# Retention's query and key projections moved into the seven-product run, kept in DRAM, with attention and retention stepped together

## The chip, the cores and the metric

One core of one Trainium2 chip runs the whole program. The metric is the device time of one launch in microseconds (us). Before the change the median of three runs is 2574.4 us (2571.2 to 2575.66).

## The reference, cut to what matters

Two transformer blocks over 1024 tokens of width 1024, in float32. The change concerns the first block's mixer:

```python
proj = h @ w_in[l]
aq, ak, av, rq, rk, rv, rg, ga, gr = jnp.split(proj, offsets, axis=-1)
att = sliding_window_attention(aq, ak, av, sinks)          # 8 heads of 64, window 128
ret = retention_chunkwise(rq, rk, rv)                      # 4 heads, key 128, value 256, chunks of 128
ret = head_group_norm(ret, ret_gn_gain[l]) * jax.nn.silu(rg)
merged = jax.nn.sigmoid(ga) * (att @ w_att_o[l]) + jax.nn.sigmoid(gr) * (ret @ w_ret_o[l])
...
# retention, per head and chunk
scores = jnp.einsum('bihd,bjhd->bhij', qi, ki) * decay_intra
o = jnp.einsum('bhij,bjhv->bihv', scores, vi) + jnp.einsum('bihd,bhdv->bihv', qi, state) * decay_q
state = decay_chunk * state + jnp.einsum('bjhd,bjhv->bhdv', ki * decay_k, vi)
```

## The kernel before, in words

Every large product is made of float32r matmuls of 128 by 128 by 512, three for each product, since each operand is split into a high and a low part (`split`, L277: ScalarE casts the high part at L279, VectorE subtracts at L281). Engines: PE is TensorE, DVE VectorE, ACT ScalarE, POOL GpSimd, and SP the queue that issues nearly all DMAs. Instructions of one engine run in program order. A tile is waited for by semaphores that the framework places.

Most projections use a seven-product (Strassen-like) form of a 2 by 2 block product. `s_run` (L504) does this for pairs of 128 output columns: seven groups of 12 matmuls (`s_group`, L496), 84 a pair, with the weights' combinations made by DVE (`s_emits`, L399) and an `ev` callback for each of the four output blocks. The activation operands of the seven products are held in `X.keep` (`Rows`, L118). Block 1 (`block1`, L772) sends 15 pairs through it: the gates RG, GA and GR, and the attention's queries and keys AQ1, AK and AQ0 (L838, L839).

Retention's queries and keys are not among them. After `s_run` each of the eight units rq0, rk0, ... rk3 is a plain product (`t_unit`, L587, with `t_group`, L573): two halves of 24 matmuls, 384 in all. For them the operand's high and low parts of a block more than the seven products need are kept (the order ending in 8, L741, and the loop at L745).

The rest is written as generators. `pump` (L232) starts `self.new` of those that stand in `self.pend`, then lets each older one take its next step, newest first. `t_group` pumps once in the middle of 24 matmuls and `t_unit` once behind them, so a step of attention or of retention comes after each 12 matmuls.

- `att1_quad` (L1272): four heads of one 128-query tile in four steps: scores (8 matmuls, then for each head a reduction on DVE, L1285, and an exponential on ACT, L1288); transposes (L1301) with copies by ACT (L1304) and DVE (L1306); the product with V (L1314); transposes back and the split of the result (L1323 to L1328). 16 quads, all of u = 0 first.
- `retention` (L1336): `vload`, eight `chunk` steps in two halves each (scores and key transpose L1355 to L1361; then output, state and statistics L1369 to L1384), and `finish` (loads of the gate rows L1394, normalisation L1397, transposes L1404, result rows L1406). `queue_retention` (L1331) puts two heads side by side, heads 0 and 1 after rk1, heads 2 and 3 after rk3.

Then the loop at L902 multiplies the attention's result by w_att_o: 16 half units of 12 matmuls (`ao`), each gated at L911 and stored, each followed by a pump. Then follows the seven-product run with w_ret_o (`d_run` at L953, evacuation `ro_evac` L937), whose operands are retention's result rows (`a_split`, L1109).

Buffers that matter: four PSUM banks for `mm`, `sc`, `po`, `tq` and `ao` (pool `pm`), three for transposes (`pt`), one for `pv`, and 43 SBUF slots of 4 KB a partition (`S`). Weights are loaded into two raw buffers (`load_raw`, L294) and split `ahead` pieces in advance in `tick` (L321).

Of the kernel before, what the change touches and what calls it, by code (L numbers as in the profile page):

```python
# [117 lines left out]
class Rows:  # L118
# [32 lines left out]
    def queue(self, c, order, kept=False):  # L151

        k = self.k
        k.d_queue(None, [(c, 0, 4, order[1:], kept)])
# [6 lines left out]
    def half(self, kt, th):  # L161
        hi, lo = self.keep[{(0, 0): 1, (1, 0): 2, (0, 1): 8, (1, 1): 4}[kt // 4, th]][kt % 4 // 2]
        return hi[:, kt % 2, :], lo[:, kt % 2, :]
# [12 lines left out]
class Kern:  # L176
# [165 lines left out]
    def t2_chunk(self, wa, ca, wb, cb, keys):  # L342

        def load(s):
            return lambda r: r.rearrange("p (k s c) -> p k s c", k=8, s=2)[:, :, s, :]
        va = wa[:, ca : ca + P].rearrange("(k p) c -> p k c", p=P)
        vb = wb[:, cb : cb + P].rearrange("(k p) c -> p k c", p=P)
        ck = self.add_chunk([(load(0), va), (load(1), vb)])
        for u, key in enumerate(keys):
            def src(hi, lo, r, u=u):  # L350
                return hi, lo, r.rearrange("p (k s c) -> p k s c", k=8, s=2)[:, :, u, :]
            self.add_piece(key, ck, [P, 8, P], src)

# [150 lines left out]
    def s_run(self, op, pairs, at={}):  # L504
# [4 lines left out]
        saved = {}  # L509
        def hoist2(i):  # L510
# [76 lines left out]
    def t_unit(self, w, X, evac, kts=range(8)):  # L587
        for half in range(2):
            ps = self.PM("mm")
            self.t_group(ps, w, X, half, kts)  # L590
            self.tick()
            evac(half, ps)
            self.pump()

# [40 lines left out]
    def plan(self):  # L635
# [49 lines left out]
    def run(self):  # L685
# [55 lines left out]
        X.queue("rv", ORD_V + (8,), kept=True)  # L741
# [3 lines left out]
        while len(X.keep) < 8:  # L745
            self.a_split(True)
            if ("rv", 8, 1) in self.a_ready:
                X.keep[8] = [self.a_ready.pop(("rv", 8, j)) for j in range(2)]
        self.flush()
# [22 lines left out]
    def block1(self, X):  # L772
# [19 lines left out]
        aq_d = {(t, th): dp.tile([P, 2, 512], F32, name=f"aq_d{t}_{th}") for t in (2, 3) for th in range(2)}  # L792
        self.dk = self.cp.tile([P, 4], F32, name="dk")

        def tables():
# [4 lines left out]
            nc.sync.dma_start(self.dk, a["c_main"][:, 9 * P :])  # L800
            alibi = [self.S(f"alibi{i}") for i in range(2)]
# [36 lines left out]
        pairs = [(f"{k}{i}", gate_ev(k, i)) for k in ("RG", "GA", "GR") for i in range(0, 8, 2)]  # L838
        pairs += [("AQ1", aq_ev(1)), ("AK", ak_ev), ("AQ0", aq_ev(0))]  # L839
        self.s_run(X.ops, pairs)  # L840
        tables()
        self.ahead = 1
# [14 lines left out]
        self.pend.append(av_tr())  # L857
        for u in range(2):
            for n in range(NT):
                self.pend.append(self.att1_quad(n, u, aq, ak, av, att))  # L860

# [3 lines left out]
        qk = []  # L865
        for h in range(4):
            qd, kT = self.S("qd"), self.S("kT")

            def q_ev(half, ps):
                nc.vector.tensor_tensor(  # L870
                    qd[:, 512 * half : 512 * half + 512].rearrange("p (c i) -> p c i", i=P),
                    ps.rearrange("p (c i) -> p c i", i=P),
                    self.dq[h][:, None, :].to_broadcast([P, 4, P]), ALU.mult)

            self.t_unit(self.get(f"rq{h}"), X, q_ev)
            if h == 0:
                for t in (2, 3):
                    aq[t] = {}
                    for th in range(2):
                        aq[t][th] = q = self.S("qst", [P, 2, 512], F32R)  # L880
                        nc.sync.dma_start(q.bitcast(F32), aq_d[t, th])
            self.t_unit(self.get(f"rk{h}"), X, lambda half, ps: nc.scalar.copy(kT[:, 512 * half : 512 * half + 512], ps))
            qk.append((qd, kT))
            if h % 2:
                self.queue_retention((h - 1, h), qk, rg_d, rows)
                self.new = 2
# [8 lines left out]
        def gload(i):  # L895
            t = self.S("tga")
            nc.sync.dma_start(t, ga_d[i])
            return t
        tga = gload(0)
        while att.missing:  # L900
            self.pump()
        for i in range(8):  # L902
            if i % 2 == 0:
                ao = self.get(f"ao{i // 2}")
            st, tg, tga = self.S("m1"), tga, gload(i + 1) if i < 7 else None
            for half in range(2):
                sl = slice(512 * half, 512 * half + 512)
                po = self.PM("ao")
                self.t_group(po, ao, att, half, range(4), cs=P * (i % 2))
                self.tick()  # L910
                nc.vector.scalar_tensor_tensor(st[:, sl], tg[:, sl], 1.0, po, op0=ALU.add, op1=ALU.mult)  # L911
                if i >= 5:
                    self.ahead = 2
                    self.a_split()
                self.pump()
            nc.sync.dma_start(m_d[i], st)
# [63 lines left out]
    def ffn1(self, X, x1_d):  # L980
# [64 lines left out]
        self.s_run(X.ops, pairs, {  # L1045
# [4 lines left out]
        X.keep.clear()  # L1050
# [221 lines left out]
    def att1_quad(self, n, u, aq, ak, av, att):  # L1272
# [24 lines left out]
        for s in range(2):  # L1297
# [33 lines left out]
    def queue_retention(self, heads, qk, rg_d, rows):  # L1331
        parts = [self.retention(h, *qk[h], rg_d, rows) for h in heads]
        for gens in zip(*parts):
            self.pend.extend(gens)

    def retention(self, h, qd, kT, rg_d, rows):  # L1336
        nc = self.nc
        v = []
# [4 lines left out]
        def vload():  # L1343
            for b in range(2):
                t = self.S("rvh", [P, 4, 256])
                nc.sync.dma_start(
# [577 lines left out]
```

## Time and profile before

| what | value |
|---|---|
| median of three runs | 2574.4 us |
| the profiled execution's own time | 2574.72 us |
| its span, first to last instruction | 2572.9 us |
| mean granted TensorE clock | 0.988 |
| PE busy | 2504.7 us (97%) |
| DVE busy | 1765.6 us (69%) |
| ACT busy | 1142.2 us (44%) |
| matmuls recorded | 11857 |

Times in the rows count from the span's first instruction. A matmul's record is longer than its share of the engine, because matmuls overlap in the array; the distance from one start to the next is what one costs. The granted clock is 1.00 at 2.4 GHz and 0.50 at 1.2 GHz.

### The profile page before, as it was taken

Reading aid. Unit: us, or ns where it says so; the run is one execution under the profiler, and the core shown is the slowest. Engines: PE = TensorE matmul, PEld = TensorE weight load, DVE = VectorE, ACT = ScalarE, POOL = GpSimd, SP = SyncE. Lnnn points to the kernel's source line nnn. Section 1 sums busy time; section 2 is a strip of 40 time slices with the busy share of each in tenths; the row PEclk is TensorE's granted clock in tenths of the full one; section 3 lists DMA queues with packets and bytes.
Section 4 is the critical chain, followed back from the end, with each engine's and each line's share of the span. In section 5 each row is a group of like instructions: output and inputs, shape, how many; then the busy total and the mean of one; then the engine's idle time right before and its main releaser. Section 6 shows DMA issues by size and latency. Waiting matters only on the chain.

```text
span 2572.9 us, 31324 instructions
## 1 busy us (share of the span) xinstructions
PE 2504.7 (97%) x11857; PEld 2073.0 (81%) x11857; DVE 1765.6 (69%) x2789; ACT 1142.2 (44%) x2068; POOL 178.7 (7%) x236
## 2 busy tenths in 40 slices
PE   7999999999999999999999999999999999899998
PEld 5888888888787888878788777888887888788886
DVE  7664456556899755555799986666558444478888
ACT  5444445412425433333333644566436555553334
POOL 1000000000002000000000300002421000000006
PEclk9999999999999999999999999999899999999999
DMA  4333333135343122233433415221242333522334
GB/s 157 104 110 103 123 103 107 39 113 185 109 186 131 66 70 87 87 130 98 174 121 131 144 49 172 102 81 51 81 160 82 104 117 103 180 108 81 115 123 147
DMA packets 178703, 291.57 MB, mean 113 GB/s; under 512 B 10168, under 2 KB 84552, under 8 KB 178552
## 3 DMA queue, kind: packets, MB, share of 16 engines
q1 hardware_dynamic: 178552, 289.57, 33.1%
q8 instruction: 93, 1.52, 0.2%
q14 instruction: 58, 0.48, 0.1%
HBM read 212.89 MB, written 80.31 MB: 114 GB/s over the span
## 4 chain that ended last, share of the span: by engine, by line
PE 78%; DVE 13%; DMA 3%; ACT 3%; issue 2%; POOL 1%; SPq 0%; DVEq 0%; ACTq 0%; POOLq 0%
PE da L1201 6%; PE a L500 6%; PE a L502 6%; PE a L501 6%; PE da L1200 6%; PE da L1199 6%; PE db L1201 3%; PE db L1200 3%; PE db L1199 3%; PE b L502 3%; PE b L501 3%; PE b L500 3%; DVE wl L281 3%; PE pv L1861 2%; DVE midl L281 2%
## 5 line engine op out<-in xcount | busy, mean ns | idle before, releaser
L500 PE MATMUL a<-midh,ws 128*128 128x512 f32 x708 | 276.8, 391 | 9.1 <-DVE f L1669 8.0
L502 PE MATMUL a<-midh,ws 128*128 128x512 f32 x708 | 276.4, 390 | 0.0
L501 PE MATMUL a<-midl,ws 128*128 128x512 f32 x708 | 276.4, 390 | 0.0
L1201 PE MATMUL da<-wh,midl 128*128 128x512 f32 x624 | 245.1, 393 | 6.6 <-DVE midl L281 6.6
L1200 PE MATMUL da<-wl,midh 128*128 128x512 f32 x624 | 244.6, 392 | 3.4 <-DVE wl L281 3.4
L1199 PE MATMUL da<-wh,midh 128*128 128x512 f32 x624 | 246.0, 394 | 0.6 <-ACT midh L279 0.6
L279 ACT CAST midh<-mt 128x1024 fp32r<-128x1024 f32 x80 | 82.9, 1036 | 244.6 <-DVE mt L1142 81.3
L1201 PE MATMUL db<-wh,midl 128*128 128x512 f32 x436 | 171.0, 392 | 3.5 <-DVE midl L281 3.5
L1200 PE MATMUL db<-wl,midh 128*128 128x512 f32 x436 | 170.8, 392 | 2.2 <-DVE wl L281 2.2
L1199 PE MATMUL db<-wh,midh 128*128 128x512 f32 x436 | 171.1, 392 | 1.4 <-ACT midh L279 1.4
L500 PEld LDWEIGHTS a<-midh,ws 128*128 128x128 f32 x708 | 133.4, 188 | 38.7 <-issue 8.9
L501 PEld LDWEIGHTS a<-midl,ws 128*128 128x128 f32 x708 | 133.5, 189 | 27.7
L502 PEld LDWEIGHTS a<-midh,ws 128*128 128x128 f32 x708 | 133.5, 189 | 27.7
L279 ACT CAST ws<-tc 128x512 fp32r<-128x512 f32 x180 | 111.4, 619 | 88.3 <-DVE tc L414 87.1
L1201 PEld LDWEIGHTS da<-wh,midl 128*128 128x128 f32 x624 | 117.8, 189 | 34.5 <-DVE midl L281 10.3
L1200 PEld LDWEIGHTS da<-wl,midh 128*128 128x128 f32 x624 | 117.9, 189 | 29.0 <-DVE wl L281 4.8
L500 PE MATMUL b<-midh,ws 128*128 128x512 f32 x360 | 140.1, 389 | 0.0
L501 PE MATMUL b<-midl,ws 128*128 128x512 f32 x360 | 140.1, 389 | 0.0
L502 PE MATMUL b<-midh,ws 128*128 128x512 f32 x360 | 140.0, 389 | 0.0
L279 ACT CAST wh<-raw 128x1024 fp32r<-128x1024 f32 x121 | 120.6, 1037 | 42.0 <-DMA raw<-in_w_ff_dram 15.2
L1199 PEld LDWEIGHTS da<-wh,midh 128*128 128x128 f32 x624 | 118.0, 189 | 26.0 <-issue 1.2
L281 DVE TENSOR_TENSOR wl<-raw,wh 128x1024 fp32r<-128x1024 f32 x117 | 136.2, 1197 | 3.6 <-ACT wh L279 3.5
(348 smaller groups left out, 5822.8 us busy)
## 6 DMA issues: line engine op xcount, KB each, us to landing
raw<-in_w_ff_dram SPq DMA_DIRECT2D x31, 1024.0 KB, 5.4
mid_d<-f SPq DMA_DIRECT2D x108, 256.0 KB, 2.1
midr<-mid_d SPq DMA_DIRECT2D x52, 512.0 KB, 6.9
raw<-in_w_in_dram SPq DMA_DIRECT2D x22, 1024.0 KB, 5.4
x<-x_d SPq DMA_DIRECT2D x24, 512.0 KB, 4.5
raw<-in_w_up_dram SPq DMA_DIRECT2D x11, 1024.0 KB, 5.6
raw<-in_w_gate_dram SPq DMA_DIRECT2D x10, 1024.0 KB, 5.5
xt<-in_x_dram SPq DMA_DIRECT2D x16, 512.0 KB, 10.9
```

Source lines behind the costliest of these rows:

```text
L279: self.nc.scalar.copy(hi, s)
L281: e.tensor_tensor(lo, s, hi.bitcast(F32), ALU.subtract)
L500: nc.tensor.matmul(ps, hi[:, i], xh, start=(first and i == 0), stop=False, skip_group_check=True)
L501: nc.tensor.matmul(ps, hi[:, i], xl, start=False, stop=False, skip_group_check=True)
L502: nc.tensor.matmul(ps, lo[:, i], xh, start=False, stop=(i == 3), skip_group_check=True)
L1199: nc.tensor.matmul(ps, xh, wh, start=(kt == 0 and p in (1, 5, 2)), stop=False, skip_group_check=True)
L1200: nc.tensor.matmul(ps, xh, wl, start=False, stop=False, skip_group_check=True)
L1201: nc.tensor.matmul(ps, xl, wh, start=False, stop=(kt == m - 1), skip_group_check=True)
L1861: nc.tensor.matmul(pv[:, 64 * x : 64 * x + 64], pT[0:w, 2 * x + e, :], vv[:, 64 * h : 64 * h + 64], start=(e == 0), stop=(e == 1))
```

## The change

- The four heads' query and key units become four pairs RQ0 to RQ3 of `s_run`, between GR and AQ1. Their `ev` (`rqk_ev`) multiplies the query block by its decay and stores both to DRAM (`rq_d`, `rk_d`); `t_unit`, `t2_chunk` and the eighth operand go.
- The decay tables are loaded at pair 11, the alibi tables at the last pair, the queries of u = 1 right behind `s_run`.
- `retention` loads keys, queries and values from DRAM in two halves (`load(0)`, and `load(1)` at chunk 2); its gate rows are loaded a step earlier. The scaled key goes from DVE to ACT, and so does the second transposed copy of `att1_quad`.
- Quads and chunks go into `pend` in threes (one quad, one chunk of each of two heads, the chunks two pumps behind), in the order half, u, n, and `self.new` is 3.
- The `ao` loop takes half 0 of all eight columns first, and starts when that half's quads are done. Until its twelfth group no weights of w_ret_o are split (`cap`).
- `s_run` drops each kept operand after its last use, in all three places that call it.

```diff
+        pairs += [(f"RQ{h}", w_in, O_RQ + P * h, O_RK + P * h) for h in range(4)]
...
-        for h in range(4):
-            self.t2_chunk(w_in, O_RQ + P * h, w_in, O_RK + P * h, [f"rq{h}", f"rk{h}"])
...
-        X.queue("rv", ORD_V + (8,), kept=True)
+        X.queue("rv", ORD_V)
...
+        def rqk_ev(h):
+
+            def ev(th, c, ps, add):
+                f, src = self.H("f"), ps
+                if add is not None:
+                    nc.vector.tensor_tensor(f, ps, add, ALU.add)
+                    src = f
+                if c == 0:
+                    nc.vector.tensor_tensor(
+                        f.rearrange("p (c i) -> p c i", i=P), src.rearrange("p (c i) -> p c i", i=P),
+                        self.dq[h][:, None, :].to_broadcast([P, 4, P]), ALU.mult)
+                elif add is None:
+                    nc.scalar.copy(f, ps)
+                nc.sync.dma_start((rk_d if c else rq_d)[h][:, 512 * th : 512 * th + 512], f)
+            return ev
...
-        self.s_run(X.ops, pairs)
-        tables()
-        self.ahead = 1
+        self.s_run(X, pairs, {11: decays, 18: tables})
+        for t in (2, 3):
+            aq[t] = {}
+            for th in range(2):
+                aq[t][th] = q = self.S("qst", [P, 2, 512], F32R)
+                nc.sync.dma_start(q.bitcast(F32), aq_d[t, th])
+        self.ahead = 2
...
-            self.t_unit(self.get(f"rq{h}"), X, q_ev)
...
-            self.t_unit(self.get(f"rk{h}"), X, lambda half, ps: nc.scalar.copy(kT[:, 512 * half : 512 * half + 512], ps))
...
+        ret = [self.retention(h, rq_d[h], rk_d[h], rg_d, rows) for h in range(4)]
+        chunks = [[ret[h][c] for h in (2 * g, 2 * g + 1)] for g in range(2) for c in range(10)]
+        quads = [self.att1_quad(4 * half + n, u, aq, ak, av, att) for half in range(2) for u in range(2) for n in range(4)]
+        lag, none = 2, iter(())
+        self.pend.extend([av_tr(), none, none])
+        for i in range(lag + 20):
+            self.pend.append(quads[i] if i < 16 else none)
+            self.pend.extend(chunks[i - lag] if i >= lag else [none, none])
+        self.new = 3
...
+        for g in range(16):
+            half, i = divmod(g, 8)
+            while any(2 * n + u in att.missing for n in range(4 * half, 4 * half + 4) for u in range(2)):
+                self.pump()
+            if i // 2 not in ao:
+                ao[i // 2] = self.get(f"ao{i // 2}")
...
+            if g >= 11:
+                self.cap = 10 ** 9
+                self.a_split()
             self.pump()
...
-            dst = pT[:, 2 * nh * s : 2 * nh * (s + 1), :]
-            if s == 0:
-                nc.scalar.copy(dst, tp[:, : 2 * nh, :])
-            else:
-                nc.vector.tensor_copy(dst, tp[:, : 2 * nh, :])
+            nc.scalar.copy(pT[:, 2 * nh * s : 2 * nh * (s + 1), :], tp[:, : 2 * nh, :])
...
+        def load(b):
+
+            t, v = self.S("rkq", [P, 2, 512]), self.S("rvh", [P, 4, 256])
+            for i, src in enumerate((rk_d, rq_d)):
+                nc.sync.dma_start(t[:, i, :], src[:, 512 * b : 512 * b + 512])
...
         def chunk(c):
...
+            if c == 2:
+                load(1)
...
-                nc.vector.tensor_scalar(sd[:, 1, :], tp[:, 1, :], self.dk[:, h : h + 1], None, op0=ALU.mult)
+                nc.scalar.activation(sd[:, 1, :], tp[:, 1, :], AF.Copy, scale=self.dk[:, h : h + 1])
```

## Rows read from the trace of the kernel before

**Rows 1.** The page's head and its line of PE (busy us, share, instructions).
```profile
span 2572.9 us, 31324 instructions
PE 2504.7 (97%) x11857; PEld 2073.0 (81%) x11857; DVE 1765.6 (69%) x2789; ACT 1142.2 (44%) x2068; POOL 178.7 (7%) x236
```

**Rows 2.** Busy time by stretch: from:to, us, each engine's busy us, PEclk, DMA share, GB/s.
```profile
107.70:394.06 286.36, 286.34 (x1264) 236.57 (x1263) 153.65 (x238) 127.53 (x220) 0.00 (x0) 1.00 0.33 108
394.06:569.00 174.94, 174.74 (x1063) 151.56 (x1062) 101.94 (x342) 64.41 (x211) 4.51 (x4) 1.00 0.24 71
569.00:644.20 75.20, 72.86 (x369) 61.90 (x367) 52.91 (x126) 15.06 (x26) 3.67 (x4) 1.00 0.57 200
659.00:684.00 25.00, 21.22 (x91) 16.56 (x90) 24.70 (x27) 6.96 (x8) 0.00 (x0) 1.00 0.10 36
684.00:691.00 7.00, 6.59 (x16) 5.19 (x17) 5.83 (x6) 3.91 (x5) 0.00 (x0) 0.53 0.00 1
1683.60:1696.30 12.70, 11.34 (x59) 9.47 (x57) 9.81 (x32) 10.37 (x31) 0.00 (x0) 0.73 0.18 58
```

**Rows 3.** Timeline of SP in the gate pairs: start us, us, instruction.
```profile
304.67 0.32 SPq L788 DMA_DIRECT2D GR_d<-g  x1
...
342.75 0.32 SPq L788 DMA_DIRECT2D GR_d<-g  x1
```

**Rows 4.** Timeline of PE, one attention step between two blocks of twelve matmuls.
```profile
428.11 0.63 PE L1263 MATMUL sc<-kst,qst 128*128 128x256 f32 x4
...
430.03 1.90 PE L1314 MATMUL pv<-av,pT 128*128 128x64 f32 x16
...
431.91 0.48 PE L581 MATMUL mm<-midh,wh 128*128 128x512 f32 x1
...
434.75 0.52 PE L1263 MATMUL sc<-kst,qst 128*128 128x256 f32 x3
```

**Rows 5.** Timeline of PE, one retention step of two heads between such blocks.
```profile
529.65 0.38 PE L1355 MATMUL tp<-qd,kT 128*128 128x128 f32 x2
...
532.72 0.58 PE L581 MATMUL mm<-midh,wh 128*128 128x512 f32 x1
...
535.65 0.38 PE L1355 MATMUL tp<-qd,kT 128*128 128x128 f32 x2
```

**Rows 6.** Timeline of DVE behind the seven-product run, up to the first quad's reductions.
```profile
394.73 0.68 DVE L810 TENSOR_TENSOR f<-a,p 128x512 f32<-128x512 f32 x1
...
398.88 1.40 DVE L1236 TENSOR_TENSOR qst<-f,qst 64x512 fp32r<-64x512 f32 x2 [0.69 <-ACT qst L1233]
...
403.79 0.34 DVE L1285 CUSTOM_DVE_ANT_0 z<-sc,alibi,nsink 128x128 f32<-128x128 f32 x1
```

**Rows 7.** Timeline of PE where the second block's attention begins.
```profile
1683.66 0.55 PE L1263 MATMUL sc<-kst,qst 128*128 128x256 f32 x1
...
1696.29 1.29 PE L1263 MATMUL sc<-kst,qst 128*128 128x256 f32 x4
```

**Rows 8.** Groups of 394 to 644 us: busy us, mean ns | idle before, releaser.
```profile
L1288 ACT ACTIVATE z<-z,nm 128x256 f32<-128x256 f32 x56 | 27.8, 497 | 33.7 <-DVE nm L1285 33.7
...
L1285 DVE CUSTOM_DVE_ANT_0 z<-sc,alibi,nsink 128x256 f32<-128x256 f32 x56 | 23.7, 480 | 28.0 <-PE sc L1268 28.0
...
L1383 DVE BATCH_NORM_STATS2 bs<-ro 128x6 f32<-128x256 f32 x32 | 13.7, 428 | 16.2 <-ACT ro L1381 16.2
...
L1381 ACT COPY ro<-po 128x256 f32<-128x256 f32 x32 | 11.9, 372 | 82.9 <-DVE st L1378 56.0 <-DVE st L1376 18.9 <-PE po L1371 8.0
...
L1378 DVE SCALAR_TENSOR_TENSOR st<-st,po 128x256 f32<-128x256 f32 x24 | 9.7, 406 | 6.3 <-PE po L1373 6.3
...
L1306 DVE COPY pT<-tp 128x512 f32<-128x512 f32 x14 | 9.2, 659 | 0.0
...
L1304 ACT COPY pT<-tp 128x512 f32<-128x512 f32 x14 | 7.9, 565 | 2.2 <-PE tp L1301 2.2
```

**Rows 9.** Timeline of PE behind the last chunk: idle time and its releaser in brackets.
```profile
640.13 0.66 PE L1404 MATMUL tp<-ident,ro 128*128 128x128 f32 x4 [1.72 <-DVE rrow L1406]
```

**Rows 10.** Timeline of DVE where the run with w_ret_o reaches its second product.
```profile
659.02 0.69 DVE L949 TENSOR_TENSOR mg<-db,mg 128x512 f32<-128x512 f32 x1 [1.51 <-PE db L1201]
```

More of the change, by code (lines that the diff above doesn't have):

```diff
@@ L502, in s_group, with s_run, op @@
             nc.tensor.matmul(ps, lo[:, i], xh, start=False, stop=(i == 3), skip_group_check=True)
-    def s_run(self, op, pairs, at={}):
+    def s_run(self, X, pairs, at={}):
         nc = self.nc
         saved = {}
+        used = dict.fromkeys(range(1, 8), 0)
+        def op(p):
+            used[p] += 1
+            ops = X.ops(p)
+            if used[p] == len(pairs):
+                del X.keep[p]
+            return ops
         def hoist2(i):
@@ L585, in t_group @@
                 self.pump()
[L587 to L593, printed above, removed]
     def m_group(self, ps, X, t, ws, mid=None):
@@ L893, in block1, with gload @@
         self.a_ok = lambda k0, p: self.ret_heads <= (2 if p == 1 else 0) if k0 == 0 else left[0] <= {1: 12, 2: 8}.get(p, 0)
-        def gload(i):
-            t = self.S("tga")
-            nc.sync.dma_start(t, ga_d[i])
-            return t
-        tga = gload(0)
-        while att.missing:
-            self.pump()
[L902 to L916, printed above, removed]
+        def gload(g):
+            half, i = divmod(g, 8)
+            t = self.S("tga", [P, 512])
+            nc.sync.dma_start(t, ga_d[i][:, 512 * half : 512 * half + 512])
+            return t
+        tga, ao = gload(0), {}
+        self.cap = next(i for i, p in enumerate(self.pieces) if p[0] == "ro:1_0")
+        for g in range(16):
+            half, i = divmod(g, 8)
+            while any(2 * n + u in att.missing for n in range(4 * half, 4 * half + 4) for u in range(2)):
+                self.pump()
+            if i // 2 not in ao:
+                ao[i // 2] = self.get(f"ao{i // 2}")
+            st, tg, tga = self.S("m1", [P, 512]), tga, gload(g + 1) if g < 15 else None
+            po = self.PM("ao")
+            self.t_group(po, ao[i // 2], att, half, range(4), cs=P * (i % 2))
+            self.tick()
+            nc.vector.scalar_tensor_tensor(st, tg, 1.0, po, op0=ALU.add, op1=ALU.mult)
+            nc.sync.dma_start(m_d[i][:, 512 * half : 512 * half + 512], st)
+            if g >= 11:
+                self.cap = 10 ** 9
+                self.a_split()
+            self.pump()
+        ao.clear()
         self.new = 1
@@ L1044, in ffn1 @@
         self.d_queue(mid_d, [(k0, k0, m, ORD_M, False) for k0, m in self.dchunks])
-        self.s_run(X.ops, pairs, {
+        self.s_run(X, pairs, {
             n - 7: self.bias_build,
@@ L1328, in att1_quad, with retention @@
         nc.vector.tensor_tensor(lo[:, :, o : o + P], tp[:, 0:2, :], hi[:, :, o : o + P].bitcast(F32), ALU.subtract)
[L1331 to L1336, printed above, removed]
+    def retention(self, h, rq_d, rk_d, rg_d, rows):
         nc = self.nc
-        v = []
+        kqv, sg = {}, []
         gc = float(np.exp(RET_LOG_G[h] * 128.0))
@@ L1370, in chunk @@
             if c > 0:
-                nc.tensor.matmul(po, qd[:, cs], st["S"], start=False, stop=True)
+                nc.tensor.matmul(po, qd, st["S"], start=False, stop=True)
             if c < 7:
@@ L1410, in finish @@
             self.ret_heads -= 1
-        return [vload()] + [chunk(c) for c in range(8)] + [finish()]
+        return [first()] + [chunk(c) for c in range(8)] + [finish()]
     def bias_build(self):
@@ L1690, in ffn2 @@
         self.d_queue(mid_d, [(k0, k0, m, ORD_M, False) for k0, m in self.echunks])
-        self.s_run(X.ops, pairs, {
+        self.s_run(X, pairs, {
             len(pairs) - 3: lambda: self.pend.append(self.d_first()),
```

77 lines of the change are left out of this document (19 added, 58 removed).

## The prediction

> **What bounds the kernel now.** I read the page's head first: PE is busy 97% of a span of 2572.9 us [rows 1]. That only says that PE always has something open, so the next view is the table by stretch. From 107.7 to 394.06 us (the 15 pairs of the seven-product run) and from 394.06 to 569 us (the plain query and key units with attention, then retention, between them) PE is busy for all but 0.2 us of each, at a granted clock of 1.00, with DVE at 54 to 58% and ACT at 37 to 45%. From 569 to 644.2 us (the `ao` half units with the rest of retention) it lacks 2.3 us, one piece of which is a 1.72 us wait for a result row of retention [rows 2, 9]. Only from 659 to 684 us does another engine bound: DVE is busy 24.7 of 25 us, PE 21.2, and the clock behind it falls to 0.53 [rows 2]. So up to 644 us a matmul less is time less, and a hole that a missing matmul leaves is time as well. The timelines of PE show why there are no holes: a step of attention takes PE 3.80 us (428.11 to 431.91), a retention step of two heads 3.07 us (529.65 to 532.72), and 12 dense matmuls stand behind each, in which DVE and ACT prepare the next step [rows 4, 5].
>
> **Removed from the dense work.** The eight plain units are 384 matmuls, 32 blocks of 12. A block takes 2.84 us behind attention and 2.93 us behind retention (431.91 to 434.75, 532.72 to 535.65), of which the first matmul's late second start, 0.09 to 0.19 us, stays with whatever follows the step instead; I take 2.75 [rows 4, 5]. That is 88.0 us.
>
> **Added to the dense work.** Four pairs. The store behind one product of a gate pair comes at 304.67 us and two pairs later at 342.75, so a pair takes 19.04 us [rows 3], four 76.2. A pair's combinations, splits and evacuations fall on DVE and ACT, which are 54% and 45% busy in that run [rows 2], and the new callbacks are of a gate's size; the cover is PE's own 19 us, and without it the excess over that would count. The saving is 88.0 - 76.2 = **11.8 us**. The 16 stores and the reloads (4 MB each way) go over queues at 33% of the engines' time [rows 2]: nothing, as long as they land in time (below).
>
> **The new start of the stage.** This is the price. Behind `s_run` nothing dense is left until the first `ao` unit, in the twelfth pump; the first seventeen pumps each start a quad. What precedes the first reductions is a tail on DVE: the last query blocks are added and split from 394.73 to 400.28 us, 6.2 us behind the end of the run at 394.06 [rows 6]. Then come a copy of V and the first reductions, and ACT's exponentials behind them. In the first four pumps PE has 6 us of work (three score groups, two transposes and half a V product; parts of the 3.80 us, the first quad being half as wide). For how long they take I use two rows. The second block begins its attention without dense matmuls: from the first scores to the fourth 12.63 us pass [rows 7], with PE's clock at 0.73 meanwhile [rows 2]. By that the loss is 12.6 - 6 = 6.6 us. The other end chains the durations through ACT: exponentials start about 7.3 us behind the run's end (DVE's 6.2, the V copy, one reduction), then four quads' exponentials (four at 0.497 us each, the first shorter) and three quads' copies (both on ACT now, 1.13 us together) in order [rows 8], about 12 us, with PE's fifth pump closing a microsecond later: 20.4 us for 10.6 us of PE work, a loss of 9.8. I take **8.5**, nearer to the chain, since it has this stage's own quads.
>
> **The pumps without a filler, six to twelve.** PE has 3.80 + 3.07 + about 0.2 = 7.1 us in each. DVE's main groups are 4 x 0.480 + 2 x (0.406 + 0.428) = 3.6 us and ACT's 4 x 0.497 + 2 x 0.565 + 2 x 0.372 = 3.9 [rows 8], to which come the short ones. From above: all of DVE's 154.9 us of the old stage, less the 9.2 us of copies that go to ACT, is 92% of a new stage of 162 us [rows 2, 8]. So PE should stay the bound, with about 0.2 us lost a pump: **1.5 us** for seven. Nothing is the low end; the high one is the rival below. The key's scaling on ACT is at most the 0.372 us of a copy twice as wide [rows 8] and lies there too.
>
> **The loads.** Keys, queries and values of two heads (2 MB) are issued behind a weight chunk (1 MB) and the queries of u = 1 (2 MB), and by the chain above the first chunk needs keys and queries some 14 us behind the run's end. I take **0.5 us**, between 0 and 3. Heads 2 and 3 load one pump ahead, behind the store of an `ao` unit; that pump has 9 us of PE work. `load(1)` has two pumps. The `ao` loop stores and loads halves, 8 issues more of each on SP at about 0.32 us [rows 3]; with 2.75 us of matmuls to each they cost nothing.
>
> **What goes, and what comes late instead.** From pump 13 on an `ao` block fills each pump and PE is the bound as now. The waits of the old tail (2.3 us short in 569 to 644 [rows 2], the largest for a result row [rows 9]) go, **-2.3**. But five `ao` blocks, not six, then stand between the last chunk and the run with w_ret_o, while heads 2 and 3 are still being normalised. DVE now idles 1.51 us before its first evacuation of the second product [rows 10]; that slack is used up, and PE waits about **1.7 us** there (0 to 3). The DVE-bound 25 us and the low clock behind them stay. The eighth operand's two casts and subtractions lie ahead of a stretch in which PE never waits: nothing. Dropping kept operands earlier in the other two runs changes which slot a load takes, not when it is issued: nothing, by at most a microsecond either way.
>
> **The sum.** -11.8 + 8.5 + 1.5 + 0.5 - 2.3 + 1.7 = -1.9 us. Against the profiled execution (2574.72 us, span 2572.9) that is 2572.8; the median of the runs is 0.3 us lower, so I predict 2572.5 us: a dense saving that the stage's own start eats. About 0.2%, 5.1 us, is what a measurement of this kernel can tell from no change.
>
> **A rule on the clock.** Twice in rows an idle stretch of PE was followed by the lower level: 0.53 in 684 to 691 us behind 3.8 us of holes, 0.73 over the second block's first 12.7 us [rows 2]. The Trainium skill (TensorE: Matmul & The Clock Gate, HAM oscillation) says that a gap between bursts of matmuls sends the array back to its lower clock, so that the next burst starts slow, and advises keeping the bursts together; the trace agrees in both places, and the rule speaks against this change. The new start has some 6 us of holes within its first 9.
>
> **Rivals.**
> - **The start is cheap.** The chain through ACT shortens if DVE's tail is over sooner, and the second block's start loses little: there 1.4 us of idle time stand in the 12.7 [rows 2]. If the start costs 3, the pumps lose nothing and the old tail's slack returns, the sum is -11.8 + 3 - 2.3 + 1 = -10.1: 2564.3 us. For it: the last raw weights' subtractions that now stand between that tail and the reductions, 400.28 to 403.79 us, go [rows 6]. Against it: PE's own work there is half of the second block's. Chance 0.30.
> - **The banks close the loop (slower).** The next quad's scores need two of four PSUM banks, and one is held by retention's output until DVE has updated the state, behind four reductions, two masks and the other head. If DVE ends each round later than PE's 7.1 us, PE waits for it every pump; it decides from a DVE round of 7.1 us. Price: DVE's round, up to 92% of 7.1 by the bound above, plus the scores' 1 us in which it cannot run, 7.5 to 8.3 us, so up to 1.2 x 7 = 8.4 us instead of 1.5, and the start at 9.8: 2572.5 + 6.9 + 1.3 = 2580.7 us. Against it: the fillers of pumps 13 to 28 hide it. Chance 0.15.
> - **The lower clock reaches into the full pumps.** One spell of 7 us at half speed (684 to 691) costs 3.5 us of dense work [rows 2]; the start's spell may end in the first full pumps: 2572.5 + 3.5 = 2576. Chance 0.10.
> - **The pairs don't run at 19.04 us.** Then the saving falls; the run lacks 0.02 us of PE in 286 [rows 2], so I give this 0.03, with 2577.
>
> **How the numbers follow.** The forecast has 0.42, rivals 0.30, 0.15, 0.10 and 0.03. Over 0.2% faster: nearly all of the first rival and a small part of the forecast, 0.33. Over 0.2% slower: most of the bank rival and small parts of the clock and pair ones, 0.17. The rest, 0.50, is no change. Range 2564 to 2581: from the cheap start to the bank loop, which leaves out about 2 in 10; the forecast's own range is 2568 to 2577.
>
> **What would show it.** In the changed profile: the run of 19 pairs ends near 470 us; the first `ao` matmul stands some 70 us later; PE is busy about half of the first 20 us behind 470, with a spell below 1.00 in it; pumps six to twelve come 7.1 to 7.4 us apart in the starts of the scores; the last chunk's products stand near 624 us, the first product with w_ret_o near 641. The prediction is wrong if the score groups come over 8 us apart or if the first full pump comes within 14 us of the run's end.

## The result and the profile after

The changed kernel takes 2587.45 us (median), the kernel before 2574.32 on the same chip: ratio 1.0057, 95% interval 1.0046 to 1.0069. Each median is of six executions, of which one took far longer (2791.74 and 4680.04 us); the other five of the changed kernel took 2584.62 to 2594.0 us, and over the fives the medians are 2586.55 and 2574.23. It is slower by 12 to 13 us where I forecast 2 us less, and it lies outside my range. Its profiled execution took 2594.0 us (span 2592.1). That one is 6.5 us above its median, so I read its stages and not its total. The page's head and its line of PE, changed kernel:

```profile
span 2592.1 us, 31389 instructions
...
PE 2505.1 (97%) x11809; PEld 2068.1 (80%) x11809; DVE 1772.2 (68%) x2791; ACT 1165.2 (45%) x2134; POOL 179.0 (7%) x236
```

PE has 48 matmuls less than in [rows 1] and is busy no less: the lower clock and longer open matmuls hide in a busy share.

The table by stretch, changed kernel (columns as in [rows 2]). The first row is what the run has become longer by, from its old end to its new one. The other cuts are the first pump with scores and both retention heads' steps in full (below: the full pump), the end of that pump, the first `ao` matmul, the last chunk, and the first product with w_ret_o.

```profile
394.06:471.41 77.35, 77.33 (x340) 63.45 (x340) 48.40 (x74) 34.50 (x58) 0.00 (x0) 1.00 0.42 122
471.41:495.03 23.62, 14.61 (x94) 12.08 (x92) 15.67 (x56) 15.65 (x50) 0.00 (x0) 0.78 0.92 328
495.03:504.35 9.32, 9.32 (x51) 8.26 (x49) 4.92 (x21) 4.34 (x16) 0.00 (x0) 0.64 0.01 2
504.35:545.98 41.63, 41.63 (x301) 37.86 (x299) 30.85 (x126) 26.98 (x94) 0.00 (x0) 1.00 0.02 7
545.98:632.47 86.49, 84.91 (x526) 74.58 (x524) 54.36 (x173) 29.75 (x97) 3.68 (x4) 1.00 0.43 147
632.47:654.20 21.73, 17.43 (x78) 13.46 (x77) 14.91 (x31) 6.27 (x7) 3.67 (x4) 0.95 0.72 253
654.20:669.00 14.80, 14.80 (x66) 12.23 (x65) 9.95 (x12) 2.71 (x4) 0.00 (x0) 0.85 0.64 233
```

Against [rows 2] the run's end moves from 394.06 to 471.41 us. No compute engine is near full in the second row: PE is open 14.61 of 23.62 us, DVE 15.67, ACT 15.65, at a mean clock of 0.78. That is a chain of waits, not a bound by one of these engines; the DMA engines, though, are busy for 0.92 of it, and no run tests by itself whether they bound it. The third row is a pump without one idle moment at a clock of 0.64. The sixth lacks 4.3 us of PE, and the first product with w_ret_o comes at 654.20, where it came at 644.2 [rows 2].

The start on PE, changed kernel (start us, us, instruction, idle before and its releaser):

```profile
473.12 0.36 PE L1249 MATMUL sc<-kst,qst 128*128 128x256 f32 x1
477.44 0.76 PE L1249 MATMUL sc<-kst,qst 128*128 128x256 f32 x3 [3.96 <-DVE f L807]
...
482.24 1.63 PE L1287 MATMUL tp<-ident,z 128*128 128x128 f32 x4 [3.32 <-ACT z L1274]
...
492.56 0.66 PE L1287 MATMUL tp<-ident,z 128*128 128x128 f32 x4 [1.74 <-ACT sd L1346]
```

Three waits, each for something else: the last product's PSUM bank, which DVE frees late (L807 is the last query blocks' addition); the first exponentials; a bank that retention's first key tiles hold until ACT has scaled the key. Behind the first two stands ACT, whose timeline has:

```profile
473.69 1.04 ACT L275 CAST wh<-raw 128x1024 fp32r<-128x1024 f32 x1 [3.09 <-DMA raw<-in_w_att_o_dram]
474.64 1.25 ACT L1219 CAST qst<-f 64x512 fp32r<-64x512 f32 x2
477.42 1.26 ACT L1219 CAST qst<-f 64x512 fp32r<-64x512 f32 x2 [1.52 <-DVE f L807]
478.70 1.05 ACT L275 CAST wh<-raw 128x1024 fp32r<-128x1024 f32 x1
481.69 0.40 ACT L1274 ACTIVATE z<-z,nm 128x128 f32<-128x128 f32 x1 [1.94 <-DVE nm L1271]
```

A cast of `ao` weights waits 3.09 us for their transfer, and the casts of the last queries are queued behind it. The first exponential starts 10.3 us behind the run's end; I had 7.3.

The end of the loop on DVE, changed kernel (timeline):

```profile
642.26 0.69 DVE L897 SCALAR_TENSOR_TENSOR m<-tga,ao 128x512 f32<-128x512 f32 x1 [4.85 <-DMA tga<-GA_d]
642.87 2.67 DVE L1382 TENSOR_SCALAR ro<-ro,mv,rw 128x256 f32<-128x256 f32 x8
...
652.62 1.42 DVE L1391 SCALAR_TENSOR_TENSOR rrow<-tp,gcol,sgr 128x512 f32<-128x512 f32 x2
```

The same moment on SP, which issues the loads and stores:

```profile
631.85 0.32 SPq L898 DMA_DIRECT2D m_d<-m  x1
632.26 1.83 SPq L1375 DMA_DIRECT2D sgr<-RG_d  x4
634.18 0.46 SPq L883 DMA_DIRECT2D tga<-GA_d  x1
636.31 0.32 SPq L898 DMA_DIRECT2D m_d<-m  x1
636.72 0.40 SPq L883 DMA_DIRECT2D tga<-GA_d  x1
...
642.98 0.34 SPq L898 DMA_DIRECT2D m_d<-m  x1
```

The gate half is loaded one unit ahead, so on SP a unit's load stands between the stores of the two units before it. The addition at 642.26 us belongs to the store at 642.98; its half is the load at 634.18, between the stores at 631.85 and 636.31. That load is issued behind four loads of gate rows (`sgr`), 2 MB, and lets DVE go 8.1 us later. Of the loop's gate halves from 600 us on, half landed within 3.7 us of their issue, as far as the profile can tell it, and the gate rows took 6.8 (view of the DMA issues, 600 to 662 us):

```profile
tga<-GA_d SPq DMA_DIRECT2D x8, 256.0 KB, 3.7
sgr<-RG_d SPq DMA_DIRECT2D x4, 512.0 KB, 6.8
```

The normalisations of heads 2 and 3 are queued behind that addition on DVE, and PE's timeline shows its wait for the rows made from them:

```profile
653.44 1.11 PE L1389 MATMUL tp<-ident,ro 128*128 128x128 f32 x4 [4.30 <-DVE rrow L1391]
```

### The profile page after: what moved, and what is told of

It reads as the page before. It is cut to its first block, busy times and chain, and to the rows that moved or that the text cites. A ratio compares the mean times of both kernels' runs of the same rounds, so it can differ in the third digit from the quotient of the medians.

```text
span 2592.1 us, 31389 instructions
## 1 busy us (share of the span) xinstructions
PE 2505.1 (97%) x11809; PEld 2068.1 (80%) x11809; DVE 1772.2 (68%) x2791; ACT 1165.2 (45%) x2134; POOL 179.0 (7%) x236
## 5 line engine op out<-in xcount | busy, mean ns | idle before, releaser
L484 PE MATMUL a<-midh,ws 128*128 128x512 f32 x772 | 301.9, 391 | 8.4 <-DVE f L1654 7.8
L485 PE MATMUL a<-midl,ws 128*128 128x512 f32 x772 | 301.4, 390 | 0.0
L486 PE MATMUL a<-midh,ws 128*128 128x512 f32 x772 | 301.3, 390 | 0.0
L275 ACT CAST ws<-tc 128x512 fp32r<-128x512 f32 x196 | 121.4, 619 | 127.1 <-DVE tc L398 125.7
L484 PEld LDWEIGHTS a<-midh,ws 128*128 128x128 f32 x772 | 145.6, 189 | 40.5 <-issue 9.5
L485 PEld LDWEIGHTS a<-midl,ws 128*128 128x128 f32 x772 | 145.6, 189 | 30.3
L486 PEld LDWEIGHTS a<-midh,ws 128*128 128x128 f32 x772 | 145.6, 189 | 30.2
L484 PE MATMUL b<-midh,ws 128*128 128x512 f32 x392 | 152.5, 389 | 0.0
L485 PE MATMUL b<-midl,ws 128*128 128x512 f32 x392 | 152.5, 389 | 0.0
L486 PE MATMUL b<-midh,ws 128*128 128x512 f32 x392 | 152.5, 389 | 0.0
L277 DVE TENSOR_TENSOR ws<-tc,ws 128x512 fp32r<-128x512 f32 x196 | 134.6, 687 | 14.4 <-ACT ws L275 11.7
L277 DVE TENSOR_TENSOR ws<-raw,ws 128x512 fp32r<-128x512 f32 x147 | 101.1, 689 | 59.4 <-ACT ws L275 58.4
```

Source lines behind the costliest of these rows:

```text
L275: self.nc.scalar.copy(hi, s)
L277: e.tensor_tensor(lo, s, hi.bitcast(F32), ALU.subtract)
L484: nc.tensor.matmul(ps, hi[:, i], xh, start=(first and i == 0), stop=False, skip_group_check=True)
L485: nc.tensor.matmul(ps, hi[:, i], xl, start=False, stop=False, skip_group_check=True)
L486: nc.tensor.matmul(ps, lo[:, i], xh, start=False, stop=(i == 3), skip_group_check=True)
```

## The experiments

Each row is one kernel; the ratio is to the kernel before on the same chip, where its median was 2573.39 to 2574.32 us. The intervals reach about 0.1%, 2 to 4 us, to either side, so a difference of 1 or 2 us between two rows shows nothing by itself.

| kernel | median us | ratio, 95% interval |
|---|---|---|
| changed | 2587.45 | 1.0057 (1.0046 to 1.0069) |
| e1 gate halves two ahead | 2582.65 | 1.0034 (1.0021 to 1.0046) |
| e2 filler of 30 matmuls | 2588.62 | 1.0051 (1.0038 to 1.0065) |
| e7 filler of 52 matmuls | 2587.77 | 1.0056 (1.0042 to 1.0070) |
| e3 head 3's pair last | 2586.92 | 1.0050 (1.0037 to 1.0062) |
| e4 `ao` weights split later | 2588.92 | 1.0064 (1.0050 to 1.0078) |
| e8 copies back on DVE | 2585.13 | 1.0044 (1.0029 to 1.0059) |
| e9 = e1 + e8 | 2578.35 | 1.0018 (1.0010 to 1.0027) |
| e5 quads in the last pair | 2586.11 | 1.0043 (1.0030 to 1.0055) |
| e6 = e5 + e1 + loads moved | 2581.87 | 1.0035 (1.0023 to 1.0048) |
| e10 = e5 + e1, loads in order | 2575.68 | 1.0005 (0.9996 to 1.0013) |
| e11 = e10 + e8 | 2576.03 | 1.0005 (0.9996 to 1.0014) |
| e13 gate rows later | 2588.98 | 1.0058 (1.0046 to 1.0071) |
| e12 = e11 + e13 | 2572.37 | 0.9998 (0.9989 to 1.0007) |
| e14 = e12 + values later | 2573.19 | 0.9991 (0.9982 to 1.0000) |
| e15 = e14 + chunks three quads behind | 2569.29 | 0.9982 (0.9974 to 0.9991) |

**The loop's tail (e1).**

```
-            st, tg, tga = ..., tga, gload(g + 1) if g < 15 else None
+            st, tg = ..., tga.popleft()
+            while g + len(tga) < min(15, g + (2 if g >= 8 else 1)):
+                tga.append(gload(g + 1 + len(tga)))
```

> Edit: from the ninth ao half unit on, the gate halves are loaded two units ahead, not one; nothing else. In the changed kernel's trace VectorE waits 4.8 us (637.4 to 642.2) for one gate half whose load was issued behind the store of the unit before; 16 normalising instructions of retention's last heads stand behind it in VectorE's order, TensorE then waits 4.47 us at 648.86 for their transposes, and a spell of 6.83 us at half clock follows (3.4 us of work). Theory 'the loop's tail is worth its stall': both go, 4.5 to 8 us less than the changed kernel's 2587.5, so 2579.5 to 2583. Rival 'VectorE bounds the 25 us behind it anyway': the stall goes and comes back in the stretch behind, within 1.5 us, 2586 to 2588.

Measured: 2582.65 us, 4.8 less, which is the first theory by its smaller end. SP's timeline, and DVE's at the same unit, e1:

```profile
625.35 0.43 SPq L883 DMA_DIRECT2D tga<-GA_d  x1
...
631.20 1.83 SPq L1377 DMA_DIRECT2D sgr<-RG_d  x4
...
637.25 0.69 DVE L899 SCALAR_TENSOR_TENSOR m<-tga,ao 128x512 f32<-128x512 f32 x1 [0.90 <-PE ao L574]
```

The half for this unit is now issued at 625.35 us, ahead of the gate rows, and DVE waits 0.90 us, for PE. One load, late by its place in a queue, was worth 4.8 us (the two intervals just touch); DVE's bound behind it did not swallow that. The edit moves the load ahead of a store as well as of the gate rows. That the gate rows held it up, and not the store, as I had assumed before the run, is read from the issue times of the changed kernel.

The Trainium skill (DMA: Bandwidth & Descriptors, Anatomy of one DMA) says that a wait on a semaphore happens on the issuing sequencer ahead of dispatch, not on the DMA engines. SP's rows of the changed kernel agree: the load at 636.72 us went out 0.4 us behind the store that had waited for the addition at 635.59.

**The clock in the start (e2, e7).** Matmuls into the V products' bank that nobody reads:

```
+        for i in range(m):
+            nc.tensor.matmul(pv, ak[0][:, 0:P], ak[0][:, 0:512], ...)
```

> Edit: 30 matmuls of 128x512 whose result nobody reads are put into the start of the stage (16 behind the first quad's scores, 14 behind the second's), where TensorE waits 4.11 and 3.62 us in the changed kernel's trace. They change no other engine's work. Theory 'the lower clock is half of the start's price': the spells at 0.50 (477.76 to 488.00 and 494.83 to 501.66) go or shrink, the second of them alone costs 3.4 us of a full pump; 3 to 5 us less than 2587.5, so 2582.5 to 2584.5. Rival 'the chain through VectorE and ScalarE sets the start whatever the clock': within 1 us of 2587.5 (or slower by what the filler overhangs, up to 2 us).

> Edit: 52 matmuls that nobody reads over the first four quads' pumps (16, 14, 12, 10), where 30 over the first two left the spell at half clock in the first full pump (492.77 to 499.60). Theory 'the second spell costs': no spell below 1.00 between 470 and 560 and the first full pump takes 7 us instead of 9.3: 2 to 3 us less than the short filler's 2588.6, so 2585.5 to 2586.5. Rival 'the chain through VectorE and ScalarE sets the start': the filler overhangs, 2588 to 2592.

The start with the long filler (e7), cut as the second and third row of the changed kernel's table:

```profile
472.02:496.70 24.68, 23.89 (x146) 19.46 (x144) 15.48 (x55) 15.70 (x50) 0.00 (x0) 1.00 0.90 315
496.70:502.93 6.23, 6.23 (x51) 5.83 (x49) 4.65 (x22) 4.18 (x16) 0.00 (x0) 1.00 0.00 0
```

And with the short one (e2):

```profile
470.40:493.70 23.30, 19.89 (x124) 15.73 (x122) 15.54 (x56) 15.61 (x50) 0.00 (x0) 0.98 0.95 333
493.70:502.60 8.90, 8.90 (x49) 8.02 (x48) 4.78 (x21) 4.36 (x16) 0.00 (x0) 0.67 0.00 1
```

In e2 PE runs at 0.98 in the first stretch, and that still takes 23.30 us, against 23.62. So the chain through DVE and ACT sets the start whatever the clock, as the rivals said. (e7 alone would not show it: there the filler itself keeps PE busy for 23.89 of 24.68 us.) The full pump takes 6.23 us in e7 instead of 9.32: the low clock does cost there, and the two stretches together give 2.0 us back (30.91 against 32.94). The totals are those of the changed kernel. The short filler left the full pump at 8.9 us.

The Trainium skill (TensorE: Matmul & The Clock Gate, HAM oscillation) says that a gap sends the next burst off at the lower clock. The pump at 0.64 behind the three waits agrees, and so does its going when they were filled; but filling the gaps gave back only those 2 us of the start's price.

**What stands ahead of the first reductions (e3, e4).** e3 puts head 3's pair last in the run; e4 holds the `ao` weights' splits back to pumps six to eight:

```
+            self.cap = next(i for i, p in enumerate(self.pieces) if p[0] == "ao0")
```

> Edit: the pair of head 3's query and key stands last in the run, behind AQ1, AK and AQ0, nothing else. Theory 'the start waits for the query splits of the last pair': VectorE then has one addition and one mask behind the run's end in place of four split subtractions and two additions, the first score reduction comes some 3 us sooner after the run's end (9.8 us in the changed kernel), and the time falls by 2 to 4 us: 2583.5 to 2585.5. Rival 'ScalarE's exponentials and copies set the start': the first reduction comes sooner, but the first full pump does not (23.6 us behind the run's end), within 1 us: 2586.5 to 2588.5.

> Edit: the first weights of the half units `ao` are cast and split in pumps six to eight, not behind the run's last products. Theory 'the weights in the tail delay the first reductions': a cast on ScalarE and two of 1.22 us on VectorE leave the path between the run's end and the first score reduction (9.8 us in the changed kernel), 1 to 3 us less: 2584.5 to 2586.5. Rival 'the start is set further on' (as the filler and the order suggest, both within 1 us): the first reduction comes sooner, the first full pump does not, 2586.5 to 2588.5; the later splits may cost the first half unit up to 2 us.

Both left the median where it was. e3's stage, from the run's end to the first `ao` matmul and on to the first product with w_ret_o:

```profile
471.40:540.12 68.72, 62.34 (x439) 56.01 (x438) 48.30 (x198) 44.78 (x156) 0.00 (x0) 0.95 0.35 123
540.12:651.04 110.92, 104.98 (x602) 90.59 (x600) 68.98 (x202) 36.05 (x104) 7.36 (x8) 0.97 0.46 163
```

The first of these took 74.57 us in the changed kernel, the second 108.22. So this stage did get shorter in the profile, by 5.9 us, with the first full pump 20.9 us behind the run's end, not 23.6: against the rival. Of the 5.9 us 2.7 were lost again before w_ret_o; the other 3 are not found in the median of five executions, and where they go stays open. e4's start, the full pump and the stretch up to 545 us:

```profile
470.43:490.59 20.16, 14.15 (x93) 11.81 (x92) 13.78 (x54) 13.67 (x48) 0.00 (x0) 0.80 0.98 332
490.59:499.41 8.82, 8.82 (x49) 7.95 (x48) 4.84 (x21) 4.35 (x16) 0.00 (x0) 0.68 0.01 2
499.41:545.00 45.59, 44.02 (x309) 39.27 (x308) 33.67 (x130) 30.02 (x98) 0.00 (x0) 1.00 0.09 30
```

Without the weights the start is 20.16 us long; I had forecast 20.4, and had not counted them. But with them split in the pumps without a filler, PE lacks 1.6 us there, and the total did not fall: part of the work was moved, not hidden.

**Copies on ACT (e8) and the two together (e9).**

```
-            nc.scalar.copy(pT[...], tp[:, : 2 * nh, :])
+            (nc.vector.tensor_copy if s else nc.scalar.copy)(pT[...], tp[:, : 2 * nh, :])
-                nc.scalar.activation(sd[:, 1, :], tp[:, 1, :], AF.Copy, scale=...)
+                nc.vector.tensor_scalar(sd[:, 1, :], tp[:, 1, :], ...)
```

> Edit: undoes one part of the change, the second copy of the probabilities and the scaling of the transposed key go back from ScalarE to VectorE. Theory 'ScalarE chains the start': the first full pump comes 1 to 3 us sooner and the filler-less pumps keep their 7.1 us: 2584.5 to 2586.5. Rival 'VectorE then bounds the pumps without a filler': seven pumps grow from 7.1 to 7.5 to 8.5 us, 3 to 10 us more: 2590 to 2597.

> Edit: the two edits that each took some microseconds away, in the changed kernel's own order: copies and key scaling back on VectorE (2585.1 us alone) and gate halves two units ahead from the ninth (2582.65 alone). Theory 'start and tail are two separate prices': they add, 2.3 + 4.8 us less than 2587.45, so 2579 to 2582. Rival 'VectorE, with the copies back, is late in the tail again': no more than the gates alone, 2582 to 2585.

e8's start and full pump by stretch:

```profile
470.46:492.91 22.45, 14.24 (x93) 11.80 (x92) 17.56 (x60) 13.84 (x45) 0.00 (x0) 0.77 0.98 343
492.91:499.11 6.20, 6.20 (x51) 5.80 (x50) 4.88 (x22) 3.35 (x13) 0.00 (x0) 1.00 0.05 15
```

The start is 1.2 us shorter, and the full pump, at full clock, 3.1 (28.65 us for both, against 32.94); the total fell by 2.3, with intervals that overlap.

The other six pumps take 41.65 us, as in the changed kernel (41.63): they did not grow with more on DVE, so the rival of a bound by DVE falls. e9, with the same edit, has a full pump of 6.2 us too. It took 2578.35 us, where the two gains by themselves would give 2580.35: start and tail are separate prices.

**A dense cover for the start (e5, e6, e10, e11).** Head 3's pair goes last, and the stage's pumps begin inside it:

```
+        self.s_run(X, pairs, {11: decays, 17: tables, 18: stage})   # stage() queues quads and chunks
```

> Edit: the order of the run above, and the stage's pumps begin inside the run's last pair (head 3's, which is needed only some 20 pumps later): V's transposes and the first quads step behind its five products of 12 matmuls each. Theory 'the start without dense matmuls is the price': the 13 us that TensorE loses between the run's end and the first full pump (23.6 us for 10.6 us of work) and the low clock in that pump (2.3 us) shrink to 2 to 5 us; 9 to 13 us less than 2587.5, so 2574.5 to 2578.5. Rival 'VectorE and ScalarE cannot take the first quads and the last pair's evacuations together': the waits move into the pair, 2 to 4 us less, 2583.5 to 2585.5.

> Edit: the quads begin in the run's last pair, the gate halves come two units ahead (both as before), the queries of u = 1 are reloaded behind the first retention loads instead of ahead of them, and the loads of heads 2 and 3 are issued one pump sooner. With the quads in the last pair TensorE still waited 3.82 + 2.19 us for the first keys and queries, 1.72 us for those of heads 2 and 3, and 4.47 us in the loop's tail. Theory 'the waits add up on TensorE': these 12 us go but for 2, from 2586 to 2575 at most and down to 2571. Rival 'the lower clock takes it back' (the kernel with the quads in the last pair had a mean clock of 0.982 to 0.984 in its unprofiled runs, 0.987 in the profiled one): waits go, half of their worth comes back, 2578 to 2582.

> Edit: quads in the run's last pair and gate halves two units ahead (as before), the loads of heads 0 and 1 one pump earlier and ahead of the queries of u = 1, the second weights of `ao` not split until the half units start (so that the 1 MB of w_ret_o are not loaded in between), and the loads of heads 2 and 3 where the changed kernel has them. Theory 'the transfers set what is left of the start': the waits of 1.55 and 2.56 us for keys and queries and the spell of 13.65 us at half clock behind them go, and so do the 4.20 us of wait and the 10.24 us spell at 558 that the earlier loads of heads 2 and 3 brought: 2572 to 2577. Rival 'what goes in waits comes back elsewhere': 2579 to 2583, as with the edits together (2581.9).

> Edit: the kernel above with copies and key scaling back on VectorE. Theory 'ScalarE is the later engine of a pump in the start': 2 to 4 us less than the kernel above, 2569 to 2575, which would be level with the kernel before (2574) or under it. Rival 'with a pair's evacuations beside it VectorE is as late': the same as the kernel above within 1.5 us, or slower.

e5 by stretch, the pair with the quads in it and what follows:

```profile
463.10:477.05 13.95, 13.95 (x86) 11.75 (x84) 11.37 (x40) 12.03 (x38) 0.00 (x0) 1.00 0.93 294
477.05:495.80 18.75, 13.22 (x90) 12.14 (x88) 10.25 (x38) 9.04 (x30) 0.00 (x0) 0.82 0.85 301
```

The pair hides the first pumps without any loss on PE, at 1.00. But the wait comes back behind it: DMA is at 0.85 to 0.93, and retention's first keys are issued behind the reloaded queries and 1 MB of w_ret_o. e5's total fell by 1.3 us only, which the intervals cannot tell from nothing (its profiled execution, 2580.71 at a mean clock of 0.987, was the best of five; the others had 0.982 to 0.984). e6 loaded heads 2 and 3 sooner and met the tail's fault again: a gate half behind 2 MB of loads, for which DVE waits 3.9 us, in a pump of 15.9 us at a clock of 0.68 of which PE lacks 4.0 (e6 by stretch):

```profile
556.00:571.90 15.90, 11.86 (x53) 10.32 (x52) 6.53 (x24) 4.11 (x14) 0.00 (x0) 0.68 0.26 93
```

With the first loads put in order and that undone, e10 and e11 are level with the kernel before: e10 within its first theory by its total, though its PE still waits 2.26 and 2.22 us for the keys and queries of heads 2 and 3, while copies on DVE (e11) no longer bring anything, as its rival had it.

**The keys of heads 2 and 3 (e13, e12, e14) and the lag (e15).**

> Edit: the changed kernel with the gate rows of retention's heads 0 and 1 (2 MB) loaded two pumps later, behind the keys, queries and values of heads 2 and 3, not ahead of them. Theory 'the burst sets the wait': the 1.6 us that TensorE waits for keys and queries at 565 us go, 1 to 2 us less than 2587.45: 2585.5 to 2586.5. Rival 'the loads are late by their own 2 MB': the wait stays within 0.5 us, 2587 to 2588, or a wait for a gate half takes its place as in the kernel with the edits together (4.2 us).

> Edit: the same on the kernel with the quads in the last pair, its loads in order, the copies on VectorE and the gate halves two ahead (2576.03). There TensorE waits 0.71 + 2.52 us for keys and queries of heads 2 and 3 and a spell of 6.83 us at half clock follows (3.4 us of work). Theory 'the burst sets the wait': both go, 3 to 6 us less: 2570 to 2573, below the kernel before by a little. Rival: the wait stays or becomes one for a gate half, 2575 to 2578.

> Edit: on the best kernel so far (2572.37), the first 512 KB of values of each head are loaded one pump behind its keys and queries, so that both heads' keys and queries come first. Theory 'the second head's keys stand behind the first head's values': TensorE's wait of 2.09 us at 556 goes, 1 to 4 us less with what the clock gives back: 2568.5 to 2571.5. Rival 'the values are then late': the wait moves one step on to the product with the values, 2572 to 2575.

> Edit: the kernel above with retention's chunks starting three quads behind the first, not two. Theory 'the first chunk meets the last pair's evacuations': the wait of 2.35 us for the bank at 479 us and the low spell behind it (10.24 us, up to 5 us of work) shrink, 2 to 5 us less than the kernel above: 2565 to 2569. Rival 'the bank is short in any pump of the start': the wait comes one pump later, and retention ends a pump later with one half unit fewer behind it: the same within 1 us or up to 4 us more, 2568 to 2573.

The gate rows ahead of the loads were not the cause: e13 kept the time, and e12, in its total 3.7 us under e11 (with intervals that overlap), still has on PE's timeline

```profile
558.19 0.46 PE L1352 MATMUL tp<-rkq 128*128 128x128 f32 x2 [1.93 <-DMA rkq<-rq_d]
```

It stands ahead of the second head's keys, which are queued behind the first head's values. With the values a pump later (e14) 0.2 us of that wait is left, though the medians of e12 and e14 cannot tell it, and e14's total lies in its rival's range. e15 starts the first chunk a pump later, to meet pumps in which the pair's evacuations are over. By stretch, its pair, what follows, the rest of the stage, and the run with w_ret_o:

```profile
462.26:476.24 13.98, 13.98 (x86) 11.79 (x85) 11.23 (x41) 9.41 (x33) 0.00 (x0) 1.00 0.93 287
476.24:492.30 16.06, 14.35 (x119) 13.17 (x118) 13.34 (x52) 8.14 (x33) 0.00 (x0) 1.00 0.83 292
492.30:631.62 139.32, 137.95 (x862) 121.20 (x860) 108.16 (x350) 50.76 (x155) 7.36 (x8) 1.00 0.39 136
631.62:669.00 37.38, 34.77 (x164) 28.13 (x163) 33.17 (x43) 10.73 (x13) 0.00 (x0) 1.00 0.38 136
```

PE lacks 1.7 us behind the pair and 1.4 in the rest, at 1.00 throughout. The 1.7 are the old wait for the bank (2.2 us in e14), one pump later, as the rival had it; what is gone in this execution is the low clock, which e14's profile has behind that wait for 10.24 us. The first product with w_ret_o stands at 631.62 us, 12.6 before that of [rows 2]. The run behind it, where DVE is busy 33.17 of 37.38 us, gives 2.6 of that back. At 2569.29 us, 4.7 or 0.18% under the kernel before, this is the one version whose whole interval lies below it. It is 0.3 us above its theory's range and within its rival's.

## Why the prediction was wrong, point by point

**The pairs were right.** 77.35 us for four; 1.15 of them is a run that was late already, since the last gate store comes at 343.95 us, not 342.75 [rows 3]. So 76.2 stands. The saving of 11.8 is not measured apart; e15, with the prices mostly gone, is 12.6 us ahead at the first product with w_ret_o. The last gate store, SP's timeline of the changed kernel:

```profile
343.95 0.34 SPq L766 DMA_DIRECT2D GR_d<-g  x1
```

**The start was mis-sized: 8.5 forecast, 13.0 measured** (23.62 us for 10.6 of work). The step that failed is "exponentials start about 7.3 us behind the run's end". I had let the raw weights' subtractions go from that tail; in fact the next weights' casts and splits stood in it, with a transfer ahead of them. The first exponential came 3.0 us later for it. Even 9.8, my high end, was short, because it was a chain of durations without queues, and 8.5 leaned off it by 1.3. e4 without these weights has my 20.4 to 0.2 us.

**The pumps without a filler were right in sum**: 9.32 + 41.63 = 50.95 us for seven, forecast 49.7 + 1.5. But the first paid for the clock (9.32; 6.23 in e7) and the others were shorter than forecast, 6.94 each. Score groups over 8 us apart, one of my signs of being wrong, came once, in that first pump. The rival of the low clock was right in its mechanism; that of the banks fell, here and in e8. Its bound on DVE was far off: 154.9 less 9.2 us is 90% of 162, not 92, and DVE was busy 35.77 of these 50.95 us, 70%.

**The loads**: 1.6 us of PE's time in 545.98 to 632.47, forecast 0.5, inside my bounds; 1.44 of them are a wait for the keys and queries of heads 2 and 3.

**The tail failed outright.** I forecast that the old waits go (-2.3) and that 8 more issues on SP "cost nothing". I had counted SP's time for them, 0.32 us each, and not what a load stands behind: 2 MB of gate rows, issued just ahead of one half, which made DVE wait 4.85 us. The sixth row lacks 4.3 us, its clock of 0.95 takes about 1.1 of 21.73, and the next row's 0.85 about 2.2 of 14.80. In e1, with that half ahead of the gate rows, DVE waits 0.90 us at this place and PE 1.69 instead of 4.30.

**The sum.** To the first product with w_ret_o I forecast 644.2 - 11.8 + 8.5 + 1.5 + 0.5 - 2.3 = 640.6; it came at 654.20. Of those 13.6 us the late run is 1.15, the start 4.5, the pumps -0.25, the loads 1.1, and the tail 5.4; some 1.7 stay unplaced. Against the kernel before, the changed one is 10.0 us late at that product, and 14.5 at the last matmul ahead of the long wait of that run: 4.5 more, where I had 1.7, and the clock behind the tail's wait makes up 2.2 of them. PE's timeline, kernel before:

```profile
680.92 0.40 PE L1199 MATMUL da<-midh,wh 128*128 128x512 f32 x1
```

and changed kernel:

```profile
695.45 0.39 PE L1185 MATMUL da<-midh,wh 128*128 128x512 f32 x1
```

What the profiled execution loses beyond that (19.3 in all) lies in code that is the same. The median is 13.1 slower, less than the 14.5: one profiled execution places the median's microseconds only to one or two. Nothing in these runs puts a price on dropping kept operands sooner.

My chances failed in the same place as the sum: three prices (start, clock, tail) were given a middle value each, or nothing, and treated as unrelated. Start and tail both rest on what an in-order queue holds up when its cover is gone, and the low clock came behind their waits, so they came out high together.

## What to carry to other kernels

When dense work is taken out of a stage, list what waits in the queues that it covered: a weight's cast ahead of the operand's, a prefetch behind 2 MB of other loads, and which of two heads' loads comes first. Price each by what is queued behind it, not by its own length, and expect the prices to rise together. If the saving is real, as here, move a piece of the dense work that remains to where the new stage starts, and then put the loads in the order of their need; by the medians the cover alone (e5) brought 1.3 us, and the order of the loads, gate halves included, 10.4 more (e10).

## What the runs showed of the hardware

The granted clock did not follow the length of a hole. At the same place of code that both kernels share, the one before waited longer and kept its clock; the changed one waited less and lost it. The matmul behind the hole, PE's timeline, kernel before:

```profile
1141.55 0.50 PE L500 MATMUL c<-zh,ws 128*128 128x512 f32 x1 [2.16 <-ACT ws L279]
```

The stretch around it, kernel before, at 1.00:

```profile
1141.00:1147.00 6.00, 5.45 (x23) 4.22 (x24) 3.70 (x6) 3.83 (x7) 0.00 (x0) 1.00 0.19 38
```

The same matmul, changed kernel:

```profile
1155.36 0.50 PE L484 MATMUL c<-zh,ws 128*128 128x512 f32 x1 [1.75 <-ACT ws L275]
```

The stretch behind it, changed kernel, with no idle time and 0.66:

```profile
1156.00:1161.00 5.00, 5.00 (x16) 3.88 (x16) 3.04 (x6) 2.54 (x5) 0.00 (x0) 0.66 0.25 59
```

The other profiles agree: in the seventeen, the wait at this place is 1.23 to 2.38 us; the clock fell behind it in nine (waits of 1.58 to 2.38) and kept its level in eight (1.23 to 2.19). What else decides it, these runs don't show.

Times differ from one execution to the next along with the clock: e14 took from 2567.08 to 2575.96 us; its three executions under 2568 had mean clocks of 0.988 to 0.991, the six above 2573 had 0.986 to 0.988. A profiled execution is one draw from that, and e5's was a lucky one.
